# Unused pieces of SBUF put the operands of the long products at one place modulo 512 bytes

## The chip, the core and the metric

One core of one Trainium2 chip runs the whole program. The metric is device time in microseconds, the median of several runs. TensorE (PE) multiplies; VectorE (DVE), ScalarE (ACT) and GpSimd (POOL) do the rest of the arithmetic; SyncE (SP) issues nearly all loads from HBM. The on-chip memory SBUF has 128 partitions. A tile begins at one byte address, the same in every partition. In this document a tile's **place** is that address modulo 512.

## What is computed

A trunk of two layers over 256 latent and 256 context tokens of width 1024. Each layer is a half-step SwiGLU FFN, a mixer (windowed attention on half the heads, retention on the other half), and a second half-step SwiGLU FFN. Every sublayer has an RMS norm before and after it, and a shift, scale and gate from a conditioning vector. The FFN, cut from the reference:

```
u = rmsnorm(h, g_pre) * (1 + scale) + shift
a, b = jnp.split(u @ wi, 2, axis=-1)
y = (jax.nn.silu(a) * b) @ wo
return h + FFN_RESIDUAL * gate * rmsnorm(y, g_post)
```

The FFN is 2816 wide. In the last layer only the latent tokens go through the mixer's output and the second FFN.

## The kernel before

**How a product is made.** Each float32 operand is split into hi (rounded to float32r) and lo (the rest), and a product is three TensorE products: hi·hi, lo·hi, hi·lo. One TensorE product has a stationary operand of 128 columns, which is loaded into the array first (512 bytes in each partition), and a moving operand of 256 or 512 columns that streams past it. A "long product" below is one with 512 moving columns.

**The products of an FFN.** Up: the stationary operand is a 128-column piece of a weight tile (`whi`, `wlo`, or `w4` for a few tiles at a sublayer's start; the trace prints `w4` as `w`). The moving operand is the normed input, `uh` or `ul`, both streams at once. Helper `uT`, lines 195 to 202, makes three products for each of 8 row tiles, into the PSUM tile `ps_up`. Down: the other way round. The stationary operand is a 128-token piece of the gated activation (`ghl`), the moving one is 512 columns of weights, and the result is `ps_dn` (lines 525 to 534). There are 11 chunks of two row tiles in each of two halves of the output. Two chunks of the second half keep their weights in the context's part of `uh` and `ul` (line 174).

```
198         hi, lo = (w[:, k, :] for w in w2)
199         mhi, mlo = (x[:, s0:s1, k, :] for x in (uh, ul))
200         nc.tensor.matmul(ps, lhsT=hi, rhs=mhi, start=(k == 0), stop=False)
...
531                    nc.tensor.matmul(y, lhsT=ghi[i][:, cs], rhs=hi[i], start=(f == 0), stop=False)
```

**The mixer** uses `uT` for projections with tokens along the columns (`ps_pj`). It uses `u_tok` (lines 204 to 215) for those with tokens on partitions (`ps_pk`) and for the output projection (`ps_wo`): there `uh` or `ul` is stationary and the weights move, as in Down. A few weight chunks of the output projection lie in tiles `wt` (line 183). Attention's products are 128 or 256 columns wide, apart from the scores: `ps_po` (line 689) has the values `vz` stationary and the softmax weights `pT` moving; `ps_ry` (line 832) has `pmh`/`pml` stationary and `vr` moving.

**What feeds TensorE.** SP loads a weight chunk (`raw`, five buffers), ACT rounds it into `whi`, and DVE subtracts to get `wlo` (lines 158 to 164, three buffers each). Between these DVE also makes the sums of the modulation vectors (line 281), dealt out in small steps by a list (`Filler`, line 288).

**Where tiles lie.** Four SBUF pools follow one another: `const`, `w` (raw, whi, wlo and the modulation weights), `act` (h, uh, ul, gates) and `t2`. Inside a pool the tags lie in the order in which they are first asked for, each as large as all its buffers, a slot rounded up to 32 bytes. The pool `t2` begins with `c_in` (64 bytes). Then comes the tag `t2k` with 26 buffers of 2048 bytes (g, the last chunks' ghl, pmh, p, wt and others). Then `ss` (384 bytes), `rstd` (320) and `adav` (64). Then the two tags `t4k0` and `t4k1` (the other ghl, w4, pT, vr; lines 49 and 50), and small tiles.

```
47        return t2.tile(shape, dt, tag="t2k", name=name, bufs=26)
50        return t2.tile(shape, dt, tag=f"t4k{which}", name=name, bufs=2)
...
160        hi = wp.tile([P, shape[0], shape[1]], R, tag="whi", name="whi", bufs=3)
161        lo = wp.tile([P, shape[0], shape[1]], R, tag="wlo", name="wlo", bufs=3)
162        nc.scalar.activation(hi, raw, AF.Copy)
163        nc.vector.tensor_sub(lo, raw, hi.bitcast(F32))
...
517                    g2 = [halves(t4k(w, [P, 2, n], R, name="ghl")) for w in range(2)]
...
519                    g2 = [[t2k([P, n], R, name="ghl") for _ in range(2)] for w in range(2)]
```

All slices that the products take are multiples of 512 bytes into their tiles, so a tile's place is that of each slice. The places in the program before:

| tiles | place |
|---|---|
| raw, whi, wlo, h, uh, ul | 192 |
| all of tag t2k (late ghl, wt, pmh, pml, qe, qo, zh, zl, p, xn) | 256 |
| all of t4k (most ghl, w4, pT, vr) | 0 |
| vz | 160 |
| ident (moving operand of transposes) | 128 |

So in Up the two operands of nearly every product begin at one place. In Down they begin at 192 and 0, or 192 and 256.

Of the kernel before, what the change touches and what calls it, by code (L numbers as in the profile page):

```python
# [8 lines left out]
F32 = mybir.dt.float32  # L9
# [6 lines left out]
P = 128  # L16
L = 2            # layers
D = 1024
KT = 8           # 128-row tiles of D
NFF = 22         # 128-row tiles of the FFN width  # L20
TOK = 512        # 256 latent tokens, then 256 context tokens
# [6 lines left out]
# Products are float32: each operand x is kept as hi + lo, both float32r (hi = x rounded  # L28
# to float32r, lo = x - hi), and a product is hi*hi + lo*hi + hi*lo.
# [3 lines left out]
def hybrid_kernel(ctx: ExitStack, tc: tile.TileContext, A: dict, out: bass.AP):  # L33
    nc = tc.nc
    pool = lambda name, bufs, **kw: ctx.enter_context(tc.tile_pool(name=name, bufs=bufs, **kw))
    const = pool("const", 1)
    wp = pool("w", 1)
    act = pool("act", 1)
    t2 = pool("t2", 1)
# [15 lines left out]
    # ---------------------------------------------------------------- constants  # L55
# [21 lines left out]
    def keep_warm(n):  # L77
        """Products of no use, where the tensor engine waits for longer than its clock stays up."""
        warm = psum([P, P], "ps_warm")
        for _ in range(n):  # L80
            nc.tensor.matmul(warm, lhsT=ident, rhs=ident, start=True, stop=True)
# [3 lines left out]
    # attention values by key tile: of both groups, hi | lo  # L85
    vz = [const.tile([P, 2, 2, 64], R, name=f"vz{t}") for t in range(4)]

    h = act.tile([P, 4, D], F32, name="h")
    # the operand on partitions of a sublayer's first product, by stream and 128-row tile; hi and lo
# [11 lines left out]
    # sums the two rows of a modulation's halves, for each of two modulations and streams  # L101
# [4 lines left out]
    def constants(anchor):  # L106
        """What the first products don't need; its loads go behind anchor."""
        dec = small([P, 16], "dec", 1)
        with tc.issue_after(anchor):
            nc.sync.dma_start(perm, A["perm"])  # L110
            tri = t2k([P, 2, P], name="tri")
            nc.sync.dma_start(tri, A["tri"])
            nc.sync.dma_start(sink, A["sink"])
            nc.sync.dma_start(edge, A["edge"])
            nc.sync.dma_start(gpost, A["gpost"])
            nc.sync.dma_start(cbc, A["c2"].to_broadcast([P, 2, D]))
            nc.sync.dma_start(dec, A["decay"])
        nc.scalar.activation(cbc, cbc, AF.Silu)
        nc.vector.tensor_copy(trib, tri)
        nc.vector.tensor_scalar_mul(negsink, sink, -1.0)  # L120

        # log_sigmoid(x) = min(x, 0) - log1p(exp(-|x|)), log1p(z) = 2 atanh(z / (2 + z))
        eb = small([P, 16], "eb", 1)
        nc.vector.memset(eb, 2.718281828459045)
        na = small([P, 16], "na", 1)
        nc.vector.tensor_scalar_mul(na, dec, -1.0)
        nc.vector.tensor_tensor(out=na, in0=na, in1=dec, op=ALU.min)
        z = small([P, 16], "z", 1)
        nc.gpsimd.tensor_tensor(out=z, in0=eb, in1=na, op=ALU.pow)
        w = small([P, 16], "wz", 1)  # L130
        nc.vector.tensor_scalar_add(w, z, 2.0)
        nc.vector.reciprocal(w, w)
        nc.vector.tensor_mul(w, w, z)
        w2 = small([P, 16], "w2", 1)
        nc.vector.tensor_mul(w2, w, w)
        acc = small([P, 16], "accz", 1)
        nc.vector.tensor_scalar(out=acc, in0=w2, scalar1=1.0 / 19, scalar2=1.0 / 17, op0=ALU.mult, op1=ALU.add)
        for n in (15, 13, 11, 9, 7, 5, 3, 1):
            nc.vector.tensor_mul(acc, acc, w2)
            nc.vector.tensor_scalar_add(acc, acc, 1.0 / n)  # L140
        nc.vector.tensor_mul(acc, acc, w)
        nc.vector.tensor_scalar_mul(acc, acc, 2.0)
        nc.vector.tensor_scalar_min(dec, dec, 0.0)
        lgf = lg.rearrange("p l d h -> p (l d h)")
        nc.vector.tensor_sub(lgf, dec, acc)
        for n, v in enumerate((-1.0, 128.0, 256.0, 384.0)):
            nc.vector.tensor_scalar_mul(lgk[:, n].rearrange("p l d h -> p (l d h)"), lgf, v)

    # ---------------------------------------------------------------- weights
    loads = []  # L150
# [15 lines left out]
    def load_w_4(src):  # L166
        """As load_w, in other tiles."""
# [6 lines left out]
    def load_w_u(src, n):  # L174
        """Two rows of 512 weight columns, in the context's part of uh and ul, which nothing else needs then."""
# [7 lines left out]
    def load_w_t(src):  # L183
        """The same, in tiles of their own."""
# [10 lines left out]
    def uT(ps, w2, k, s0, s1):  # L195
        """ps += w.T u of streams s0.., row tile k."""
# [7 lines left out]
    def u_tok(ps, hi, lo, k, t):  # L204
        """ps += u.T w of token tile t, row tile k; w of 512 columns."""
# [9 lines left out]
    # ---------------------------------------------------------------- adaLN  # L215
    gdram = {}

    def ada_done(l, m, v):
        """Of modulation m, without its bias: v[:, s, k], columns on partitions."""
# [22 lines left out]
    def ada_slice(j):  # L242
        """256 columns of layer 0's first shift and scale, on the tensor engine; rows 64m + 32i + s of its result
        hold the sum over the i-th half of c for modulation m and stream s."""
# [22 lines left out]
    behind = [None]   # the sums below go behind this instruction, their loads behind that one  # L267
    start = [None]

    def ada_steps(l, m):  # L270
        """One modulation vector of both streams: sums along the free axis."""
# [17 lines left out]
    class Filler:  # L289
# [3 lines left out]
        def later(self, n, do):  # L293
            """Runs do after n more steps."""
            self.due.append([n, do])
# [34 lines left out]
    # ---------------------------------------------------------------- norms  # L330
# [7 lines left out]
    def pre_scale(t):  # L338
        """rmsnorm of token tile t of h, without its gain."""
# [15 lines left out]
    def pre_norm(sub, s):  # L355
        """For stream s: u = rmsnorm(h) * (1 + scale) + shift, transposed, as hi and lo."""
# [20 lines left out]
    def post_half(y, gates, t, half, part):  # L377
        """Of one half of a token tile: its sum of squares, and its product with the gate; after the second half
        also the tile's 1 / rms."""
# [11 lines left out]
    def post_norm(parts, t, then):  # L391
        """h += gate * rmsnorm(y) for token tile t."""
# [7 lines left out]
    def token_tiles(nt, half, mms, ys, gates, parts, nxt):  # L400
        """The end of a sublayer's last product, token tile by token tile; mms(t): the rest of tile t's products.
        After the second half, the sublayer's own end, and the next one's start: nxt is its number, or "out"."""
# [23 lines left out]
    # ---------------------------------------------------------------- FFN  # L426
    def ffn(l, name, sub, streams, fill, nxt):
# [10 lines left out]
        def first():  # L438
            """The first pairs: the latent tokens before the context's."""
# [26 lines left out]
        def first_of_all():  # L466
            """The first pairs of layer 0, by row tiles as their modulation comes."""
            for t in range(4):
                pre_scale(t)
            xn = [[xns.pop(2 * s), xns.pop(2 * s + 1)] for s in range(2)]  # L470
# [39 lines left out]
        for half in range(2):  # L510
# [26 lines left out]
            # the last chunks go token tile by token tile  # L537
# [15 lines left out]
    # ---------------------------------------------------------------- mixer  # L553
    def mixer(l, last):
# [10 lines left out]
        # -- projections, in steps of a few products; each then runs `done` on its result  # L565
        def proj_T(ct, n, done):
            """128 columns of w_in, on partitions."""
# [8 lines left out]
        def proj_tok(c0, n_t, done):  # L576
            """512 columns of w_in for token tiles 0..n_t, tokens on partitions."""
# [9 lines left out]
        def roped(ps, n, which, then, scale=1.0):  # L587
            """Float32 copy of a projection, its latent tokens rotated; then(copy, n) follows."""
# [17 lines left out]
        def hi_over_lo(qf, n):  # L606
            """For each head of a pair: rows 0-63 hi, rows 64-127 lo."""
# [9 lines left out]
        def twice(qf, n):  # L617
            """For each head of a pair: hi in rows 0-63 and 64-127, and lo likewise."""
# [12 lines left out]
        # -- attention  # L631
# [14 lines left out]
        def scores(g, qt, hh):  # L646
            """Softmax of one head's token tile against its keys."""
# [35 lines left out]
        def weighted(g, qt):  # L683
# [7 lines left out]
            # rows 0-63 hold the products with hi, rows 64-127 those with lo  # L691
# [9 lines left out]
        def proj_first():  # L701
            """Keys, the first queries and values, latent tokens before the context's."""
# [26 lines left out]
        # -- retention's projections, among attention's heads  # L729
        qrs, krs, vr, sg = [], [], [], []  # L730

        def ret_values(pss):
            # [tokens, head, hi | lo]
# [43 lines left out]
        # -- retention  # L777
        def decay(hd):
            """Weights [key of two blocks, query] of head hd."""
            lf, lb = lg[:, l, 0, hd:hd + 1], lg[:, l, 1, hd:hd + 1]  # L780
            k = lambda n, d: lgk[:, n, l, d, hd:hd + 1]
            # one sequence: exp((q - s) lf) for q >= s, exp((s - q) lb) for s > q
# [7 lines left out]
            # context key s to latent query q, through the states of both directions:  # L790
            # exp((q + 256 - s) lf) + exp((256 - q + s) lb)
# [74 lines left out]
        # -- output projection; its first half's attention part goes among retention's heads  # L866
# [24 lines left out]
        def wout(steps, then=()):  # L891
            """Products (half, chunk, token tile); the weights of the next chunks are loaded ahead."""
# [9 lines left out]
        # its products among the heads: so many before a head's end, before its transposition, and after it  # L902
# [44 lines left out]
    # ---------------------------------------------------------------- the trunk  # L947
# [38 lines left out]
def _layout(np, inp):  # L986
    """The inputs in the order in which the chip reads them."""
# [43 lines left out]
```

## Time and profile before

| what | value |
|---|---|
| runs of the kernel | 1711.91, 1714.29, 1715.02 us |
| median | 1714.29 us |
| span of the profiled execution | 1707.8 us |
| median less that span | 6.5 us |
| PE busy | 98% of the span |
| DVE, ACT, DMA queue q1 | 69%, 44%, 43.9% |

The profiled execution's time from launch to end is not listed apart from its span; the 6.5 us stand for what lies around the span. Time in the profile runs from the span's start. PE's busy time counts products that overlap: a long product's own duration is about 390 ns, while the next one starts well before it ends. The pace is therefore read from the starts, or from the count of products in a stretch.

### The profile page before, as it was taken

To read this page: it belongs to the slowest core of one execution; us is meant where nothing else is said; L and a number is where in the kernel's file an instruction comes from. 1 tells how busy PE (TensorE), PEld (TensorE's weight loads), DVE (VectorE), ACT (ScalarE), POOL (GpSimd) and SP (SyncE) were. 2 spreads that over 40 slices of the span, in tenths; PEclk is the share of its full clock that TensorE was granted. 3 is DMA by queue.
4 is the path that set the end of the run, shared out by engine and by line. 5 is a ranking of instruction groups with operands and counts; after the bars stand their busy time and mean duration, and the time that the engine had idled before them with its cause. 6 is when DMAs were issued, how large, how long until landed. Compare 5 with 4: busy or idle time off the path is not lost.

```text
span 1707.8 us, 23653 instructions
## 1 busy us (share of the span) xinstructions
PE 1680.4 (98%) x8632; PEld 1407.9 (82%) x8632; DVE 1180.3 (69%) x2625; ACT 746.4 (44%) x1299; POOL 45.7 (3%) x75
## 2 busy tenths in 40 slices
PE   8999999999999999999999999999999999989998
PEld 5788888788778788888887898888887888889986
DVE  3699995396898879982345689962347689865466
ACT  4322223355787663222234452222244578754454
POOL 1000000001000110000000000000000100000000
PEclk9999999999999999999999999999999999999999
DMA  7677674262112136662323437752324222335553
GB/s 273 228 234 256 230 239 142 83 201 77 62 50 99 68 106 228 228 231 103 99 88 114 145 126 230 237 185 99 99 87 142 75 93 87 116 134 183 185 185 112
DMA packets 89270, 254.40 MB, mean 149 GB/s; under 512 B 10560, under 2 KB 11056, under 8 KB 89024
## 3 DMA queue, kind: packets, MB, share of 16 engines
q1 hardware_dynamic: 88416, 251.16, 43.9%
q0 software_dynamic: 736, 1.72, 0.3%
q8 instruction: 68, 1.11, 0.3%
q14 instruction: 50, 0.41, 0.1%
HBM read 251.74 MB, written 1.10 MB: 148 GB/s over the span
## 4 chain that ended last, share of the span: by engine, by line
PE 79%; DVE 8%; DMA 3%; ACT 3%; issue 2%; POOL 1%; DVEq 0%; POOLq 0%; ACTq 0%
PE ps_up L200 13%; PE ps_up L201 13%; PE ps_up L202 13%; PE ps_dn L531 8%; PE ps_dn L533 8%; PE ps_dn L532 8%; DMA rawa<-in_ada_w 3%; DVE junk L281 3%; DVE wlo L163 2%; PE ps_pj L200 1%; PE ps_pj L201 1%; PE ps_pk L210 1%; PE ps_pj L202 1%; PE ps_pk L212 1%; PE ps_po L689 1%
## 5 line engine op out<-in xcount | busy, mean ns | idle before, releaser
L162 ACT ACTIVATE whi<-raw 128x1024 fp32r<-128x1024 f32 x297 | 314.7, 1060 | 773.2 <-PE ps_up L201 497.0
L163 DVE TENSOR_TENSOR wlo<-raw,whi 128x1024 fp32r<-128x1024 f32 x297 | 362.8, 1222 | 292.8 <-ACT whi L162 287.9
L200 PE MATMUL ps_up<-uh,whi 128*128 128x512 f32 (+1 forms) x1400 | 501.9, 359 | 2.5 <-DVE uh L373 2.4
L202 PE MATMUL ps_up<-uh,wlo 128*128 128x512 f32 (+1 forms) x1400 | 501.9, 359 | 0.5 <-DVE wlo L163 0.3
L201 PE MATMUL ps_up<-ul,whi 128*128 128x512 f32 (+1 forms) x1400 | 501.7, 358 | 0.0
L281 DVE SCALAR_TENSOR_TENSOR junk<-rawa,cbc 128x512 f32<-128x512 f32 x512 | 325.7, 687 | 28.0 <-DMA rawa<-in_ada_w 27.1
L200 PEld LDWEIGHTS ps_up<-uh,whi 128*128 128x128 f32 x1400 | 264.9, 189 | 43.1 <-DVE uh L373 3.6
L202 PEld LDWEIGHTS ps_up<-uh,wlo 128*128 128x128 f32 x1400 | 265.1, 189 | 40.2 <-DVE wlo L163 1.7
L201 PEld LDWEIGHTS ps_up<-ul,whi 128*128 128x128 f32 x1400 | 265.2, 189 | 38.6 <-DVE ul L374 0.8
L532 PE MATMUL ps_dn<-whi,ghl 128*128 128x512 f32 x560 | 221.3, 395 | 0.0
L533 PE MATMUL ps_dn<-wlo,ghl 128*128 128x512 f32 x560 | 221.3, 395 | 0.0
L531 PE MATMUL ps_dn<-whi,ghl 128*128 128x512 f32 x560 | 220.1, 397 | 0.0
L531 PEld LDWEIGHTS ps_dn<-whi,ghl 128*128 128x128 f32 x560 | 104.7, 188 | 27.0 <-ACT ghl L521 2.5
L532 PEld LDWEIGHTS ps_dn<-whi,ghl 128*128 128x128 f32 x560 | 105.3, 188 | 25.5 <-DVE ghl L522 0.2
L533 PEld LDWEIGHTS ps_dn<-wlo,ghl 128*128 128x128 f32 x560 | 105.3, 188 | 25.2
L436 DVE TENSOR_TENSOR g<-g,ps_up 128x512 f32<-128x512 f32 (+1 forms) x92 | 55.1, 599 | 82.2 <-PE ps_up L202 78.2
L521 ACT ACTIVATE ghl<-g 128x512 fp32r<-128x512 f32 (+1 forms) x176 | 92.2, 565 | 27.9 <-DVE g L436 18.7
L522 DVE TENSOR_TENSOR ghl<-g,ghl 128x512 fp32r<-128x512 f32 (+1 forms) x176 | 102.9, 619 | 1.7 <-ACT ghl L521 1.0
L200 PE MATMUL ps_pj<-uh,whi 128*128 128x256 f32 (+1 forms) x168 | 58.6, 349 | 0.0
L201 PE MATMUL ps_pj<-ul,whi 128*128 128x256 f32 (+1 forms) x168 | 55.9, 333 | 0.1
L202 PE MATMUL ps_pj<-uh,wlo 128*128 128x256 f32 (+1 forms) x168 | 55.6, 331 | 0.0
L371 ACT ACTIVATE uf<-ps_tr,shT,scT 128x256 f32<-128x256 f32 x88 | 41.5, 573 | 13.4 <-PE ps_tr L367 9.0
(220 smaller groups left out, 1963.0 us busy)
## 6 DMA issues: line engine op xcount, KB each, us to landing
raw<-in_ffn_wi SPq DMA_DIRECT2D x176, 512.0 KB, 3.5
rawa<-in_ada_w SPq DMA_DIRECT2D x256, 256.0 KB, 3.2
raw<-in_ffn_wo SPq DMA_DIRECT2D x88, 512.0 KB, 3.3
raw<-in_w_in SPq DMA_DIRECT2D x20, 512.0 KB, 3.6
raw<-in_ada_w SPq DMA_DIRECT2D x16, 512.0 KB, 5.1
raw<-in_w_in_t SPq DMA_DIRECT2D x16, 512.0 KB, 3.2
raw<-in_w_out SPq DMA_DIRECT2D x16, 512.0 KB, 3.3
gate<-gd SPq DMA_DIRECT2D x10, 512.0 KB, 4.1
```

The lines of the kernel that those rows point to most:

```text
L162: nc.scalar.activation(hi, raw, AF.Copy)
L163: nc.vector.tensor_sub(lo, raw, hi.bitcast(F32))
L200: nc.tensor.matmul(ps, lhsT=hi, rhs=mhi, start=(k == 0), stop=False)
L201: nc.tensor.matmul(ps, lhsT=hi, rhs=mlo, start=False, stop=False)
L202: nc.tensor.matmul(ps, lhsT=lo, rhs=mhi, start=False, stop=(k == KT - 1))
L281: nc.vector.scalar_tensor_tensor(out=junk, in0=wr[i], scalar=1.0, in1=cbc[:, st, 512 * i:512 * i + 512], op0=ALU.mult, op1=ALU.mult, accum ...
L436: nc.vector.tensor_mul(gs, gs, b)
L521: nc.scalar.activation(g2[0][i], g[2 * c + i], AF.Copy)
L522: nc.vector.tensor_sub(g2[1][i], g[2 * c + i], g2[0][i].bitcast(F32))
L531: nc.tensor.matmul(y, lhsT=ghi[i][:, cs], rhs=hi[i], start=(f == 0), stop=False)
L532: nc.tensor.matmul(y, lhsT=glo[i][:, cs], rhs=hi[i], start=False, stop=False)
L533: last = nc.tensor.matmul(y, lhsT=ghi[i][:, cs], rhs=lo[i], start=False, stop=(f == NFF - 1))
```

## The change

Three tiles are asked for that nothing writes or reads. Besides, comments and docstrings are taken out, which changes no instruction.

```
     vz = [const.tile([P, 2, 2, 64], R, name=f"vz{t}") for t in range(4)]
 
+    const.tile([P, 120], F32, name="pad")
+    t2.tile([P, 112], F32, name="pad2", tag="pad2", bufs=1)
+
     h = act.tile([P, 4, D], F32, name="h")
...
         def first_of_all():
             for t in range(4):
                 pre_scale(t)
+            t2.tile([P, 64], F32, name="pad3", tag="pad3", bufs=1)
             xn = [[xns.pop(2 * s), xns.pop(2 * s + 1)] for s in range(2)]
```

`pad` takes 480 bytes at the end of `const`, behind vz. `pad2` takes 448 bytes at the front of `t2`, before c_in. `pad3` takes 256 bytes in `t2`, behind `ss` and `rstd` (first asked for in `pre_scale`) and before `adav` and `t4k`.

## Rows read from the trace of the kernel before

**Rows 1.** The page's first part: busy time, share of the span, instructions, by engine

```profile
PE 1680.4 (98%) x8632; PEld 1407.9 (82%) x8632; DVE 1180.3 (69%) x2625; ACT 746.4 (44%) x1299; POOL 45.7 (3%) x75
```

**Rows 2.** The page's fourth part: the chain that ended last, by engine

```profile
PE 79%; DVE 8%; DMA 3%; ACT 3%; issue 2%; POOL 1%; DVEq 0%; POOLq 0%; ACTq 0%
```

**Rows 3.** PE's groups by line and shape: names (moving, stationary), count, busy, mean ns

```profile
L200 PE MATMUL ps_up<-uh,whi 128*128 128x512 f32 x984 | 383.6, 391 | 2.5 <-DVE uh L373 2.4
L531 PE MATMUL ps_dn<-whi,ghl 128*128 128x512 f32 x560 | 220.1, 397 | 0.0
...
L531 PE MATMUL ps_dn<-uh,ghl 128*128 128x512 f32 x56 | 22.1, 396 | 0.0
...
L200 PE MATMUL ps_up<-uh,w 128*128 128x256 f32 x64 | 18.1, 286 | 0.0
...
L200 PE MATMUL ps_pj<-uh,w 128*128 128x256 f32 x32 | 9.2, 286 | 0.0
...
L210 PE MATMUL ps_wo<-wt,uh 128*128 128x512 f32 x20 | 7.9, 395 | 0.0
...
L200 PE MATMUL ps_up<-uh,w 128*128 128x512 f32 x8 | 3.2, 395 | 0.0
```

**Rows 4.** Stretch of Up, instructions on ps_up alone: us, busy (count) PE, PEld, DVE, ACT

```profile
1020.00:1220.00 200.00, 200.00 (x883) 165.41 (x883) 12.35 (x18) 10.99 (x19) 1.00 0.53 176
```

**Rows 5.** Stretches of three Downs, all work: us, PE, PEld, DVE, ACT, POOL, clock, DMA, GB/s

```profile
288.00:403.00 115.00, 115.00 (x493) 92.28 (x492) 71.89 (x127) 49.30 (x80) 1.66 (x3) 1.00 0.40 130
870.00:985.00 115.00, 115.00 (x493) 92.25 (x492) 64.12 (x98) 49.68 (x80) 1.65 (x3) 1.00 0.35 115
...
1642.00:1692.00 50.00, 50.00 (x214) 39.80 (x214) 37.08 (x60) 32.73 (x61) 0.00 (x0) 1.00 0.49 158
```

**Rows 6.** Timeline of PE, products of Up: first and last of 15 (start, duration)

```profile
699.74 0.39 PE L200 MATMUL ps_up<-uh,whi 128*128 128x512 f32 x1
...
702.91 0.39 PE L202 MATMUL ps_up<-uh,wlo 128*128 128x512 f32 x1
```

**Rows 7.** Timeline of PE, products of Down: first and last of 15

```profile
899.65 0.40 PE L532 MATMUL ps_dn<-whi,ghl 128*128 128x512 f32 x1
...
902.91 0.40 PE L531 MATMUL ps_dn<-whi,ghl 128*128 128x512 f32 x1
```

**Rows 8.** Timeline of PE, Up with w4 as weights: first and last of six

```profile
57.14 0.39 PE L200 MATMUL ps_up<-uh,w 128*128 128x512 f32 x1
...
58.31 0.39 PE L202 MATMUL ps_up<-uh,w 128*128 128x512 f32 x1
```

**Rows 9.** Timeline of PE, output projection with whi and wlo: first and last of 18

```profile
599.02 0.39 PE L210 MATMUL ps_wo<-whi,uh 128*128 128x512 f32 x1
...
602.88 0.39 PE L212 MATMUL ps_wo<-wlo,uh 128*128 128x512 f32 x1
```

**Rows 10.** Timeline of PE, output projection with wt: first and last of 12

```profile
608.62 0.40 PE L210 MATMUL ps_wo<-wt,uh 128*128 128x512 f32 x1
...
611.14 0.39 PE L212 MATMUL ps_wo<-wt,uh 128*128 128x512 f32 x1
```

**Rows 11.** Timeline of PE, 256 columns: with whi (first, last of 19); with w4 (of 21)

```profile
1539.75 0.28 PE L201 MATMUL ps_up<-ul,whi 128*128 128x256 f32 x1
...
1541.91 0.28 PE L201 MATMUL ps_up<-ul,whi 128*128 128x256 f32 x1
...
414.65 0.28 PE L200 MATMUL ps_pj<-uh,w 128*128 128x256 f32 x1
...
417.00 0.28 PE L202 MATMUL ps_pj<-uh,w 128*128 128x256 f32 x1
```

**Rows 12.** Timeline of PE, the eight products with vz stationary, and the next product

```profile
531.13 1.11 PE L689 MATMUL ps_po<-pT,vz 128*128 128x256 f32 x8
532.08 0.28 PE L812 MATMUL ps_rs<-zh,qe 128*128 128x256 f32 x1
```

**Rows 13.** Stretch at the last layer's second norm: us, PE busy (count), clock, DMA, GB/s

```profile
1509.00:1512.50 3.50, 2.99 (x14) 0.50 0.03 13
```

More of the change, by code (lines that the diff above doesn't have):

```diff
@@ L86, in hybrid_kernel @@
     vz = [const.tile([P, 2, 2, 64], R, name=f"vz{t}") for t in range(4)]
+    const.tile([P, 120], F32, name="pad")
+    t2.tile([P, 112], F32, name="pad2", tag="pad2", bufs=1)
     h = act.tile([P, 4, D], F32, name="h")
@@ L469, in first_of_all @@
                 pre_scale(t)
+            t2.tile([P, 64], F32, name="pad3", tag="pad3", bufs=1)
             xn = [[xns.pop(2 * s), xns.pop(2 * s + 1)] for s in range(2)]
```

## The prediction, made before the changed kernel was run

> **What bounds the kernel now.** I read the engines first. TensorE is busy for 98% of the span, and no other engine comes near it [rows 1]. The chain of waits says the same from the end: 79% of the span is TensorE work that followed on TensorE work [rows 2]. The products by shape show where that work is: the lines L200 to L202 of Up each issue 984 long products, the lines L531 to L533 of Down each 560 with weights in whi and wlo and 56 with weights in uh and ul [rows 3]. So Up has 3 x 984 = 2952 of these, Down 3 x (560 + 56) = 1848.
>
> Then the pace. A product's duration (about 390 ns) is no pace, since the next one starts before it ends; the distance between starts is. In Up, 883 products fill 200 us, 226.5 ns each [rows 4], and 14 steps of the timeline take 702.91 - 699.74 = 3.17 us, 226.4 ns each [rows 6]. In Down, 493 products fill 115 us, 233.3 ns each, with no idle TensorE [rows 5], and 14 steps take 902.91 - 899.65 = 3.26 us, 232.9 ns each [rows 7]. Both have 512 columns, the same type and the full clock. Down is 6.5 to 6.8 ns slower per product, and I take 6.6.
>
> What differs? In Up both operands lie at place 192. In Down the moving one lies at 192 and the stationary one at 0 or 256. It could also be the form of the product, since Down swaps weights and activations. Two more groups separate these. The same line of Up with w4 as weights (stationary at 0, all else alike) needs 58.31 - 57.14 = 1.17 us for five steps, 234 ns each [rows 8]. The output projection, which has Down's form but with both operands at 192, needs 602.88 - 599.02 = 3.86 us for 17 steps, 227.1 ns each [rows 9]. The pace follows the places and not the form. A third difference has a third price: with wt moving at 256 and uh stationary at 192, 11 steps take 611.14 - 608.62 = 2.52 us, 229.1 ns each [rows 10]. So 226.5 is the best of the three levels seen, and it is the one with equal places.
>
> **The change, part by part.** No instruction, wait or transfer is added, removed or reordered. What moves is addresses. `pad` adds 480 bytes ahead of the pools w and act, so 192 becomes 192 + 480 = 672, place 160: raw, whi, wlo, uh, ul. Pool t2 now starts at 160 too; `pad2` (448) and c_in (64) are exactly 512 bytes, so t2k goes from 256 to 160. The 26 buffers of 2048 bytes change nothing; `ss` (384), `rstd` (320), `pad3` (256) and `adav` (64) add up to 1024, so t4k goes from 0 to 160. vz was at 160 and stays. All operands of the float32r products are then at 160.
>
> *Down.* 1848 products go from unequal to equal places. 1848 x 6.6 ns = 12.2 us, all of it on the path: TensorE does not wait in these stretches [rows 5]. If equal places bought only the middle level, 229.1 ns [rows 10], it would be 1848 x 4.2 = 7.8 us.
>
> *Up with w4, output projection with wt.* 3 x 8 = 24 long products at 6.6 ns less [rows 3, 8] are 0.2 us; 3 x 20 = 60 at 229.1 - 226.5 = 2.6 ns less [rows 3, 10] are 0.2 us.
>
> *256 columns.* Here the sign turns. With equal places 18 steps take 2.16 us, 120.0 ns each; with w4 at 0 twenty steps take 2.35 us, 117.5 ns each [rows 11]. 3 x (64 + 32) = 288 such products [rows 3] lose 2.5 ns, 0.7 us in all. Attention's products with vz, stationary at 160 and moving at 0, take 0.95 us for eight, 118.8 ns each [rows 12]; 160 of them at 120 lose 0.2 us.
>
> *Products at the new place.* The 2952 of Up, and those of the mixer that were equal, keep equal places but begin at 160 in place of 192. No row has both operands there. From one side the cost is nothing, since the rows so far go by the difference of the two places; from the other side they could go up to the 233.3 of Down, 6.8 ns each. I take nothing: the nearest row, with one operand at 160, is not above the 120.0 of an equal pair [rows 12].
>
> *Other engines, loads.* VectorE, ScalarE and the DMA queue read and write the same bytes at other addresses. I cost this at nothing, because TensorE covers it: in Down VectorE is busy for 71.89, 64.12 and 37.08 us of stretches of 115, 115 and 50 us, and the DMA engines for half the time at most [rows 5]. Even the tightest, 37.08 of 50 us, leaves room when the 50 become 48.6. If this cover were gone, weights would come late next.
>
> *The clock.* [...] I take 0.
>
> The sum: -12.2 - 0.2 - 0.2 + 0.7 + 0.2 = -11.7 us. The profiled execution's span of 1707.8 would become 1696.1. The median of the runs is 6.5 us more than that span, as work before and after it would be, so 1714.3 - 11.7 = 1702.6 us.
>
> The rows that give two prices to one line, by the place of the weights alone [rows 6, 8], say that the place matters. [...]
>
> **The rivals.** (a) Nothing happens. Either the pools do not move as I added them up (a tile that nobody writes might take no room), or Down's pace comes from something else that its operands share, and 233.3 stays. For it: in Down every product is unequal, so Down itself has no counterexample. Against it: rows 8 and 9 show both levels in other places. Time: 1714.3, apart from rounding. [...]
>
> (b) The place itself counts, not the difference alone: 192 is a multiple of 64, and 160 is not. If an operand that begins at half of 64 bytes costs the moving stream what unequal places cost now, the 2952 long products of Up, equal today, rise to Down's 233.3, by 2952 x 6.8 = 20.1 us, and Down gains nothing: 1714.3 + 20.1 = 1734 (the mixer's few left aside). It decides from 12.2 / (1848 + 2952) = 2.5 ns per long product upwards: beyond about 229 ns at the new place the kernel is slower than before. For it: no row has a moving operand at 160. Against it: vz at 160 as stationary operand costs nothing that can be seen [rows 12].
>
> (c) A part of the gain: Down falls to the 229.1 of the wt rows alone. 1714.3 - 7.8 + 0.5 = 1707.
>
> **How the numbers follow.** A measurement of this kernel tells about 0.2%, 3.4 us, from no change. The forecast with its full gain has 0.75, rival (c) 0.05, (a) 0.08, (b) 0.12. Faster takes the forecast and (c) with a little of (b), where the cost at 160 is under 1.8 ns: 0.81. Same is (a): 0.08. Slower is the rest of (b): 0.11. The forecast alone reaches from 1698.5 (2 us of clock regained, and 2 us for the spread of single runs) to 1706. I extend the upper end through (c) with its own spread to 1710; past it lie (a) and most of (b), together 0.2. The point is the forecast, 1702.6.
>
> **What would show it.** Right: steps of 226 to 227 ns on L531 to L533, the four Downs shorter by 3.5, 3.5, 3.5 and 1.7 us, the Ups unchanged, and L200 with w at 256 columns up from 117.5 to 120 ns. Wrong by (a): Down still alternates around 233. Wrong by (b): the lines of Up move off 226.5. Wrong in the cover: TensorE idle in Down, with a wait on wlo or a load ahead of it.

## The result and the profile after

The changed kernel takes 1700.94 us (median of four runs, 1700.11 to 1701.61), the kernel before 1713.1 us beside it (1711.73 to 1715.02). The ratio is 0.993, with a 95% interval from 0.9918 to 0.9942: 12.2 us less, where 11.7 were forecast.

The same program ran: as many instructions, DMA packets and bytes. The page's first part, after, against [rows 1]; every engine is busy as long as before, apart from PE:

```profile
PE 1671.2 (98%) x8632; PEld 1408.6 (83%) x8632; DVE 1179.5 (69%) x2625; ACT 746.8 (44%) x1299; POOL 45.8 (3%) x75
```

The products of Up and Down by line and shape, after, against [rows 3] (all line numbers are three or four higher now). The duration of a product in Down fell from 397 to 391 ns, that in Up stayed at 391:

```profile
L203 PE MATMUL ps_up<-uh,whi 128*128 128x512 f32 x984 | 384.0, 391 | 2.5 <-DVE uh L376 2.4
...
L535 PE MATMUL ps_dn<-whi,ghl 128*128 128x512 f32 x560 | 216.9, 391 | 0.2
```

The pace, in stretches of Up (on ps_up alone, as [rows 4]) and of the first Down (PE alone: us, busy, count, clock, DMA share, GB/s), after:

```profile
1018.00:1218.00 200.00, 200.00 (x883) 165.39 (x883) 12.33 (x18) 10.89 (x19) 1.00 0.54 176
...
290.00:403.00 113.00, 112.95 (x498) 1.00 0.42 135
```

Up does 883 products in 200 us, exactly as in [rows 4], although everything now lies at 160. Down does 498 in 113 us, 226.9 ns each; in [rows 5] it was 493 in 115 us. A count takes in the one or two products that the ends of a stretch cut, so a pace read from it can lie up to half a nanosecond under the steps themselves. The timeline of Down, after, the same 14 steps as in [rows 7], now 902.57 - 899.40 = 3.17 us, 226.4 ns each:

```profile
899.40 0.39 PE L535 MATMUL ps_dn<-whi,ghl 128*128 128x512 f32 x1
...
902.57 0.39 PE L537 MATMUL ps_dn<-wlo,ghl 128*128 128x512 f32 x1
```

The output projection with wt takes 610.43 - 608.16 = 2.27 us for ten steps, 227 ns, against 229.1 [rows 10]. The products of 256 columns with w4 take 416.56 - 414.76 = 1.80 us for fifteen steps, 120.0 ns, against 117.5 [rows 11]: this is the one group that became slower.

```profile
608.16 0.39 PE L213 MATMUL ps_wo<-wt,uh 128*128 128x512 f32 x1
...
610.43 0.39 PE L214 MATMUL ps_wo<-wt,ul 128*128 128x512 f32 x1
...
414.76 0.28 PE L205 MATMUL ps_pj<-uh,w 128*128 128x256 f32 x1
...
416.56 0.29 PE L205 MATMUL ps_pj<-uh,w 128*128 128x256 f32 x1
```

The first Up and the first Down as whole stretches, before (us, PE busy and count, clock, DMA share, GB/s):

```profile
21.00:283.50 262.50, 261.43 (x1190) 0.99 0.68 229
283.50:408.70 125.20, 125.20 (x546) 1.00 0.37 122
```

and after:

```profile
21.00:286.20 265.20, 262.41 (x1190) 0.99 0.69 226
286.20:408.20 122.00, 121.95 (x546) 1.00 0.39 125
```

Down gives 3.2 us. The first Up gets 2.7 us longer, with more idle PE (2.8 against 1.1 us). That is most likely not the change's doing. In this stage DVE is busy for 206.91 of the 265.2 us and waits 13.4 us for the loads of the modulation weights (10.8 us before), and in the profiles of the kernels below whose Up has equal places its length is anything from 264.4 to 267.6 us, against 262.8 before and 265.8 after. With before's differences of place kept (the first experiment below), the first Down begins at 286.3 us after the span's start, against 283.6 in the profiled execution of before. Of the kernel before there is only this one profile. So the two spans, 1707.8 and 1699.1, differ by 8.7 us only, while the medians of the runs differ by 12.2.

### The profile page after: what moved, and what is told of

Read it like the earlier page. It is cut to its first block, busy times and chain, and to the rows that moved or that the text cites. A ratio compares the mean times of both kernels' runs of the same rounds, so it can differ in the third digit from the quotient of the medians.

```text
span 1699.1 us, 23653 instructions
## 1 busy us (share of the span) xinstructions
PE 1671.2 (98%) x8632; PEld 1408.6 (83%) x8632; DVE 1179.5 (69%) x2625; ACT 746.8 (44%) x1299; POOL 45.8 (3%) x75
## 4 chain that ended last, share of the span: by engine, by line
PE 80%; DVE 7%; ACT 3%; DMA 3%; issue 2%; POOL 1%; DVEq 0%; POOLq 0%; ACTq 0%
PE ps_up L203 14%; PE ps_up L205 14%; PE ps_up L204 14%; PE ps_dn L535 8%; PE ps_dn L536 8%; PE ps_dn L537 8%; DMA rawa<-in_ada_w 3%; DVE junk L284 2%; DVE wlo L166 2%; PE ps_pj L203 1%; PE ps_pj L204 1%; PE ps_pk L213 1%; PE ps_pj L205 1%; PE ps_pk L215 1%; PE ps_po L693 1%
## 5 line engine op out<-in xcount | busy, mean ns | idle before, releaser
L205 PEld LDWEIGHTS ps_up<-uh,wlo 128*128 128x128 f32 x1400 | 265.2, 189 | 43.7 <-DVE wlo L166 5.1
L537 PE MATMUL ps_dn<-wlo,ghl 128*128 128x512 f32 x560 | 217.9, 389 | 0.0
L536 PE MATMUL ps_dn<-whi,ghl 128*128 128x512 f32 x560 | 217.9, 389 | 0.0
L535 PE MATMUL ps_dn<-whi,ghl 128*128 128x512 f32 x560 | 216.9, 391 | 0.2
L438 ACT ACTIVATE g<-ps_up 128x512 f32<-128x512 f32 (+1 forms) x92 | 47.0, 511 | 0.0
```

Source lines behind the costliest of these rows:

```text
L205: nc.tensor.matmul(ps, lhsT=lo, rhs=mhi, start=False, stop=(k == KT - 1))
L536: nc.tensor.matmul(y, lhsT=glo[i][:, cs], rhs=hi[i], start=False, stop=False)
L537: last = nc.tensor.matmul(y, lhsT=ghi[i][:, cs], rhs=lo[i], start=False, stop=(f == NFF - 1))
```

## Experiments

Two theories stood against each other. By the first, the pace of a long product depends on the difference of its operands' places. By the second, place 160 itself is good. Both fit the changed kernel, since it moves everything to one place and that place is 160.

**The first piece alone**

```
-    t2.tile([P, 112], F32, name="pad2", tag="pad2", bufs=1)
...
-            t2.tile([P, 64], F32, name="pad3", tag="pad3", bufs=1)
```

> Only the 480 bytes ahead of the pools w and act are kept; weights, uh and ul lie at 160, the tag t2k at 224, t4k at 480. So every place is 32 less than before the change, and the differences between operands are those of before (64 and 320). Theory 1, the difference of the two places counts: as the kernel before, within 0.2% (about 1713 us); Down at 233 ns per long product, Up at 226.5. Theory 2, place 160 itself is what helps: about half of the gain or more comes back in the products whose moving operand lies at 160, so Down falls towards 229 and the time to about 1705.

Measured: 1711.5 us beside 1713.43 us, ratio 0.9991, interval 0.9982 to 1.0. The gain is gone. PE in 70 us of the first Down, this kernel:

```profile
295.00:365.00 70.00, 70.00 (x301) 1.00 0.38 113
```

**The two pieces in t2 alone**

```
-    const.tile([P, 120], F32, name="pad")
```

> Only the two pieces inside t2 are kept; weights, uh, ul, t2k and t4k all lie at 192, vz stays at 160. Theory 1 (difference): the whole gain, 1700 to 1702 us, Down at 226.7 ns. The 160 products of attention with vz may differ by 1 ns, under 0.2 us. Theory 2 (place 160): no gain or a part of it, 1706 us or more.

Measured: 1702.72 us, ratio 0.9938, interval 0.9923 to 0.9953. The gain is all there. The same stretch:

```profile
295.00:365.00 70.00, 69.95 (x308) 1.00 0.37 112
```

301 products against 308 in the same 70 us: with unlike places Down is slow at 160 as at 192, with like places it is fast at 192 as at 160. The second theory falls. The 480 bytes in `const` bring nothing that can be measured.

**Up made unequal**

```
-    t2.tile([P, 112], F32, name="pad2", tag="pad2", bufs=1)
+    t2.tile([P, 64], F32, name="pad2", tag="pad2", bufs=1)
...
+    act.tile([P, 48], F32, name="pad4")
     h = act.tile([P, 4, D], F32, name="h")
```

> As the changed kernel, with 192 more bytes ahead of h, uh and ul, so that these lie at 352 and all else at 160. Now Up is unequal by 320 (stationary less moving, the difference that most of Down had before), Down is equal except for the chunks kept in uh and ul. Theory 1: Up's 2952 long products rise from 226.7 to 233.3 ns, +19.5 us; the 216 of ps_pj with 512 columns +1.4, the 168 of Down in uh and ul +1.1; the 1536 products of 256 columns fall from 120 to 117.5 ns, -3.8 us; 624 of ps_pk and ps_wo at a difference not yet seen, 0 to +4. Sum +18 to +22: 1719 to 1723 us. Rival: the price belongs to Down's form or to the weights' tiles, and Up does not move: 1701 to 1706 us.

Measured: 1711.46 us, ratio to the kernel before 0.9991 (0.9982 to 1.0001), so 10.5 us over the changed kernel and not 18 to 22. The pace moved as expected. A stretch of the third Up (on ps_up alone) and one of the last Up, where all products have 256 columns, this kernel:

```profile
1024.00:1224.00 200.00, 200.00 (x858) 161.01 (x857) 12.36 (x18) 10.40 (x18) 1.00 0.54 175
...
1530.00:1640.00 110.00, 110.00 (x973) 110.00 (x972) 8.86 (x21) 7.68 (x21) 1.00 0.59 190
```

858 long products in 200 us are 233.1 ns each, against 883 at equal places. So the price is not Down's alone. Two things kept the sum small. First, 973 products of 256 columns in 110 us are 113.1 ns each, far under the 117.5 that I had taken from [rows 11]. Second, part of the first Up's price hid in idle time that was there anyway. PE from 60 to 285 us, the changed kernel and then this one:

```profile
60.00:285.00 225.00, 222.83 (x977) 1.00 0.70 228
...
60.00:285.00 225.00, 225.00 (x966) 1.00 0.70 229
```

Of the 1056 x 6.4 = 6.8 us that its long products cost, 2.2 went into this idle time; what is left is no more certain than the length of that stage. From the first to the last product of each stage, against the changed kernel, the first Up grew by 3.2 us, the second by 5.1, the third by 5.9; the last shrank by 6.2. For the second Up the sum is 960 x 6.4 = 6.1 us of long products less 192 x 6 = 1.2 us of short ones.

**Other differences between Down's operands**

```
-    t2.tile([P, 112], F32, name="pad2", tag="pad2", bufs=1)
+    t2.tile([P, 120], F32, name="pad2", tag="pad2", bufs=1)
...
-            t2.tile([P, 64], F32, name="pad3", tag="pad3", bufs=1)
+            t2.tile([P, 88], F32, name="pad3", tag="pad3", bufs=1)
```

That is for differences of 32 (t2k) and 128 (t4k). For 256 and 448 the sizes are 48 and 112 elements, for 192 and 384 they are 32 and 112.

> As the changed kernel, with t2k 32 bytes and t4k 128 bytes past place 160. Read from the trace, not from the time: the steps of Down with ghl in t4k (difference 128) and in t2k (32), and of the 256-column products with w4. If places count modulo 64 or 128, the steps at 128 are 226.7 ns; if modulo 256 or 512, about 229 to 233. At 32: 226.7 if anything under 64 bytes is the same place, over it if not. Time: 1701 us in the first case, up to 1713 in the other.

> As the changed kernel, with t2k 256 bytes and t4k 448 bytes past place 160. Steps of Down in the trace: 448 was seen with wt at 229 to 230 ns, so 229 to 230 is expected again where ghl is in t4k; at 256, if the pace has a period of 256 bytes, 226.7, and 229 to 233 if only full 512 counts. A step under 226.7 anywhere would say that equal places are not the best.

> As the changed kernel, with t2k 192 bytes and t4k 384 bytes past place 160. Steps of Down: at 192, the difference that ps_pk and ps_wo had with uh moved away, 229 to 230 ns; at 384 not seen yet, 229 to 233 if only equal places give 226.7. Time 1706 to 1713 us.

Measured, one run each: 1710.03, 1703.52 and 1712.9 us, beside 1713.43 for the first and 1712.96 for the other two. What counts here is the mean distance between the starts of neighbouring products of one kind and one difference, from the trace of each kernel (steps over 273 ns for 512 columns and over 167 ns for 256 are left out as pauses). The difference is the stationary operand's place less the moving one's, modulo 512:

| difference | modulo 256 | 512 columns: steps, ns | kernel, products |
|---|---|---|---|
| 0 | 0 | 1825, 227.0 | changed, Down |
| 256 | 0 | 1825, 227.0 | the next experiment, Down |
| 32 | 32 | 292, 232.6 | 32 and 128, Down from t2k |
| 64 | 64 | 292, 233.5 | before, Down from t2k |
| 320 | 64 | 1478, 233.4 | before, Down from t4k |
| 320 | 64 | 2936, 233.3 | Up made unequal, Up |
| 128 | 128 | 1478, 232.3 | 32 and 128, Down from t4k |
| 384 | 128 | 1478, 232.5 | 192 and 384, Down from t4k |
| 192 | 192 | 292, 230.0 | 192 and 384, Down from t2k |
| 448 | 192 | 1478, 229.0 | 256 and 448, Down from t4k |

No difference gives less than equal places. But pairs that are the same modulo 256 have one pace, to about a nanosecond. In the kernel with 256 and 448 the products at 256 had 227 ns as their commonest step, though a mean of 228.4 over short stretches. The next experiment has longer ones.

**Everything of t2 apart by 256**

```
-    t2.tile([P, 112], F32, name="pad2", tag="pad2", bufs=1)
+    t2.tile([P, 48], F32, name="pad2", tag="pad2", bufs=1)
```

> As the changed kernel, with the first piece in t2 cut to 192 bytes, so that t2k and t4k lie at 416, exactly 256 past weights, uh and ul at 160. Theory, period 256: the pace goes by the difference modulo 256 and this kernel is as fast as the changed one, 1700 to 1702 us, Down at 226.7 to 227.2 ns. Rival, period 512, the steps at 256 seen so far being an accident of short stretches: Down at 229 to 233 ns, 1705 to 1713 us.

Measured: 1702.11 us beside 1714.55 us, ratio 0.9936, interval 0.9913 to 0.9959. The first Down of this kernel, 309 products in 70 us:

```profile
295.00:365.00 70.00, 69.95 (x309) 1.00 0.39 116
```

So the pace repeats every 256 bytes for the differences that were run (32 has no partner, 288 was not run). "Modulo 512" in the change asks for more than is needed.

**A version that goes further.** Equal places gave the shortest steps for 512 columns (227.0 ns) and not for 256 (120.0 ns, against 113.1 with Up made unequal). In the last layer's second FFN all 1056 products of Up have 256 columns, and nothing else uses the normed input there. It can therefore be written further on inside uh and ul, while all long products stay equal:

```
+            for i, x in enumerate((uh, ul)):
+                x = x.rearrange("p s k c -> p (s k c)")[:, 48:48 + KT * LAT]
+                U[i] = x.rearrange("p (s k c) -> p s k c", s=1, k=KT)
             pre_norm(2, 0)
```

(`uT` and the pre-norm use `U`, which is `[uh, ul]` until then.)

> The changed kernel with one thing more: for the last layer's second FFN the normed input is written 192 bytes further on inside uh and ul, so that its 1056 products of 256 columns have operands that differ by 320, and all long products stay equal. Two paces were seen at that difference for 256 columns, 113.4 and 117.8 ns, against 120.0 when equal. At 113.4: 1056 x 6.6 = 7.0 us less than the changed kernel, 1694 us. At 117.8: 2.3 us less, 1698.6 us. Rival, that the fall seen with all of uh and ul moved had another cause: 1701 us.

> The changed kernel itself, on the same chip as the version that goes further: 1700 to 1702 us, Down at 226.7 ns, Up with 256 columns at 120.0 ns.

Measured, on one chip beside 1712.96 us: 1697.61 us, ratio 0.9913 (0.9899 to 0.9926), for the version, and 1701.71 us, ratio 0.9936 (0.9923 to 0.995), for the changed kernel again. The version is 4.1 us faster by the medians; the intervals overlap by a hair (0.9923 to 0.9926), and its slowest run, 1700.38 us, is just under the fastest of the changed kernel there, 1700.45. A stretch of the last Up (on ps_up alone), the version:

```profile
1515.00:1625.00 110.00, 110.00 (x973) 110.00 (x972) 8.84 (x21) 7.68 (x21) 1.00 0.59 191
```

and the changed kernel again:

```profile
1515.00:1625.00 110.00, 110.00 (x919) 110.00 (x919) 8.43 (x20) 6.99 (x20) 1.00 0.57 180
```

110 us hold 973 products against 919, 113.1 against 119.7 ns. The pace was the better one of the two expected, but the time was not: 7.0 us less were forecast for it. In the profiles the last Up did shrink by 6.5 us from first to last product (127.5 to 121.0); why the medians differ by 4.1 only stays open. The profiled execution of the version had a first Up 1.8 us longer than that of the changed kernel. To see whether a difference of 192 modulo 256 is steadier, the input was moved by 64 bytes in place of 192:

```
-                x = x.rearrange("p s k c -> p (s k c)")[:, 48:48 + KT * LAT]
+                x = x.rearrange("p s k c -> p (s k c)")[:, 16:16 + KT * LAT]
```

> As the version with the last layer's normed input moved inside uh and ul, by 64 bytes in place of 192 (difference 448, that is 192 modulo 256). The 84 products of ps_pj at 448 all ran at 113.4 ns, so 113.4 is expected for nearly all 1056 and the time of the version with 192 bytes, 1694 to 1698 us. Rival: at this difference too both paces occur, and the stretch falls to 117.8 ns: 1699 us.

Measured: 1700.59 us beside 1714.55 us, ratio 0.992 (0.9902 to 0.9937). The same stretch holds 936 products, 117.5 ns each:

```profile
1515.00:1625.00 110.00, 110.00 (x936) 110.00 (x935) 8.03 (x20) 7.34 (x20) 1.00 0.57 182
```

The expectation fell and its rival came in. At this difference the products of `ps_pj` had kept 113.4 ns in the kernel with 256 and 448 (85 steps); here 1046 steps kept 117.8. So both paces occur at 448 too. The last Up took 125.6 us, against 121.0 with 192 bytes. In time the two cannot be told apart: the intervals of their ratios, each beside the kernel before on its own chip, overlap for the most part.

## Why the prediction was right

**The bound.** TensorE was the bound (98% of the span before and after), and Down's products were slower than they need be: right. Down's steps went from 233.4 to 227.0 ns and Up's stayed.

**Down, -12.2 us forecast.** Its steps fell by 6.4 ns, 1848 x 6.4 = 11.8 us. By stages, from first to last product, three Downs gave 3.2 us each and the last 1.3, 11.0 in all, where 3.5 and 1.7 were forecast. The term was 1.2 us too large. About 0.4 of that is the step, 6.4 ns and not 6.6. Most of the rest is that I multiplied the difference of steady steps by every product: the few steps over 273 ns in the four Downs, at pauses and beside the short transposes, did not shrink but grew, from 10.6 us in all (18 steps) to 11.3 (19).

**The small terms.** wt and the long products with w4 became faster by less than half a microsecond, as said. The short products with w4 lost 2.2 ns each (117.8 to 120.0), 288 x 2.2 = 0.6 us, where 0.7 was said. Those with vz did not lose: their mean step was 119.6 ns before and 119.4 after.

**The new place, taken as nothing.** Right: Up does 883 products in 200 us at 160 as at 192, and with everything at 192 the second experiment gives the same gain. Rival (b) falls with that.

**Cover.** PE waited 2.1 us for wlo in Up, against 0.3 before, and not in Down, where it was idle for 0.2 us in all. The waits lie in the first Up, where DVE is busy for 78% of the stage, against 66, 67 and 53% of the other three Ups. With before's differences of place (the first experiment) PE waited 1.4 us for wlo there, so the wait does not go with the places, and Down's cover held.

**The clock.** The stretch ahead of the last Up, after, where [rows 13] showed 0.50 throughout:

```profile
1502.00:1505.50 3.50, 2.88 (x15) 0.66 0.05 21
1505.50:1507.00 1.50, 1.50 (x11) 0.65 0.00 0
```

In both kernels TensorE had been idle for 4.4 us just before (until 1509.51 us before, until 1502.62 after). After the change a granted clock of 0.50 held for a part of these stretches only: it came at another point and was shorter, from about 1503.1 to 1506.5 us, against 1507.5 to 1514.3 us before. The forecast's range counts on up to 2 us of clock regained. No run shows that term: from the end of the idle time to the last product of that Up, 130.4 us became 129.9, 0.5 us less.

**The base.** One step was wrong without harm: that the 6.5 us between span and median lie around the span. In the run that was profiled after the change the time is 1700.97 us and the span 1699.1, so 1.9 us lie around it. Before's profiled execution would then have taken about 1709.7 us, less than any of the timed runs; it was a short one, as its first Up shows. The sum was made against the median, so the forecast did not lean on this.

**The number.** That 11.7 us came so near to 12.2 is in part luck. Down's term was 1.2 us too large, and a difference of two medians is no finer than that: in another session the same two kernels differed by 11.3 us (1712.96 and 1701.71). Of the 1.7 us between the forecast 1702.6 and the measured 1700.94, 1.2 lie in the kernel before, which took 1713.1 us this time and not 1714.3.

**The rivals.** (a) fell: the pace of the same products changed with nothing but addresses. The trace holds no addresses, but the paces in all experiments fit the places as added up. Down's steps took 233.4 ns with its operands 320 or 64 apart and 227.0 ns at one place. (c) fell, since Down went to 227.0 and not 229.1.

Why the pace goes by the difference of two addresses is not settled. The runs show that it repeats every 256 bytes for the differences that were run (227.0 ns at 0 and 256, 233.5 and 233.4 ns at 64 and 320) and that it depends on the number of columns: a difference of 320 costs 6.4 ns with 512 of them and saves 2 to 6.6 ns with 256. They do not show where in the chip it arises, and nothing was tried on that. The records of the weight loads (PEld) do not tell: they are 188 ns long in Down before and after.

## What to carry to other kernels

Where TensorE's products follow one another without a gap, compare the distance of starts between groups of one shape. Two levels in one kernel, where the operands' addresses differ and all else is alike, were worth nearly 3% of these products here (227.0 against 233.4 ns), for a few hundred unused bytes. Put both operands of 512-column products at one place modulo 256 (227.0 ns here, against 229.0 to 233.5 at the other differences); this is shown for float32r products that each load their stationary operand, and for no other type. Don't carry that to 256 columns, where equal places gave the slowest steady pace seen, 120.0 ns against 113.1 to 117.9.

## What was not expected

Products of 256 columns have two steady paces at one and the same difference. At 320 they ran at 117.8 ns in the kernel before and at 113.4 in the version that goes further (1045 steps). In the kernel with Up made unequal the same groups did both: 113.4 at the second Up's start and 117.8 at the third's. At 448 it was 117.8 in the version moved by 64 bytes, and the kernel with 256 and 448 did both within one stage: in its second Up, 36 products with w4 in a row have 113.3 ns (from 628.48 us on), then come 16 transposes, and the next unbroken row of 48 such products (from 641.49 us on) has 117.9. Equal places gave 120.0 nearly always. What decides between the two was not found; that it is how a stretch begins would be a guess, which no run tests. Whether it can change between executions of one program is not known, since only one execution of each version was profiled. The spread of the version's runs, 4.1 us, is no sign of it: the two pieces in t2 alone spread over 4.3 us.

Relations that hold for 512 columns thus say little about 256: the difference that costs most there (64 modulo 256, +6.4 ns) is among the best here (-2 to -6.6 ns).
